# First FFN of a two-layer flow step: block sums moved among the products, a NAT split moved, norm factors in one step

## The chip, the cores and the metric

The program runs on one core of a Trainium2 chip. The metric is the device time of one execution in microseconds (us). The core has a matrix engine (TensorE, PE in the rows; PEld is its weight load), a vector engine (VectorE, DVE), an activation engine (ScalarE, ACT), a general engine (GpSimd, POOL) and a queue that issues transfers (SyncE, SP). [...]

## The reference, cut to what matters

Two layers; each adds half an FFN, a mixer of three attentions (MLA, differential, neighbourhood = NAT) and half an FFN again to `x`, for 128 context and 512 latent tokens of width 1024. The weights are the same for both kinds of token; the shifts, scales and gates come from a conditioning vector and differ.

```
def half_ffn(x, g, shift, scale, gate, w_gate, w_up, w_down):
    h = rmsnorm(x, g) * (1.0 + scale) + shift
    return x + 0.5 * gate * ((silu(h @ w_gate) * (h @ w_up)) @ w_down)

for l in range(2):
    sh1, sc1, g1, sh2, sc2, g2, sh3, sc3, g3 = split(silu(c) @ w_ada[l] + b_ada[l], 9)
    x = half_ffn(x, ffn1_norm[l], sh1, sc1, g1, ffn1_w_gate[l], ffn1_w_up[l], ffn1_w_down[l])
    h = modulate(rmsnorm(x, mix_norm[l]), sh2, sc2)
    x = x + g2 * (concat(MLA(h), DIFF(h), NAT(h)) @ w_out[l])
    x = half_ffn(x, ffn2_norm[l], sh3, sc3, g3, ffn2_w_gate[l], ffn2_w_up[l], ffn2_w_down[l])
y = rmsnorm(x, final_norm)
```

## The kernel before

All 640 tokens lie along the free axis and the 1024 features on 8 tiles of 128 partitions (`x[d]`). Each matrix product in float32 accuracy is three products of rounded operands: operands are split into a high part (a cast on ACT) and a low part (a subtraction on DVE), `mm3` multiplies high by high, high by low and low by high. Weights come in slabs of 512 KB (`raw`, 4 buffers) through the SP queue; `W.get` splits them a number of slots ahead (`W.la`).

An FFN works on two halves of 320 tokens (g = 0, 1). Its first pairs of columns are computed plainly (`plain`, `gu`: 8 x 3 products of 320 columns each). All further pairs are computed by a scheme that replaces eight block products by seven (`seven`: A11, S2, S1, S3, A12, S4, A22). It needs sums of blocks of the activations, T1 to T4, made by `Boundary.blocks(k)` for k = 0 to 3: four sums on DVE and four splits (ACT cast, DVE subtraction) for each k, 32 DVE instructions of 320 columns in all. `plain` calls them after its first half. After each chunk of pairs `down` adds the down-projection to `x`; its results and those of `seven` are read from PSUM by DVE.

The first FFN of layer 0 has an opening of its own, since nothing is loaded yet: for each d from 0 to 7 `begin(d)` computes shift and scale of that feature tile from 1 MB of weights (`begin_sums`: 16 small products, `begin_vectors`: the column sums by `sel` into the PSUM tile `shift`, then `ada_bias` on DVE), applies them to the normed input (`begin_input` in three steps: product with the norm factor; shift and scale and cast; low part), and `first(k)` puts the products of one feature tile behind the preparation of the next. In this stage every instruction is held to program order on its engine (`e.pin`). The modulated input y is a temporary here, so `blocks` first rebuilds it for this FFN as high + low: 16 additions on POOL.

Besides, the modulation of the later stages is computed as background on DVE (`BG`): 112 steps during the first FFN, each of which reads one 256 KB load with two reductions of 512 columns. `BG.tick` earns `RATES[0]` of a step at each product of `seven` and each part of `down`, and three times that (`EARLY`) after each `gu` of the first FFN.

In the mixer a planner (`Plan`) orders chains of work by estimated times. `prompt_n(i)` ends with `finish_o`, the split of one NAT output of 640 columns (ACT cast, DVE subtraction); it waits until 11 units have begun and the projections ckv, cq, d0, d1, dv are done. `mla_v` (named mv) multiplies the compressed keys by one weight slot.

`Norm.stats` turns token sums of squares into factors: a reciprocal root on POOL and a diagonal matrix by one DVE instruction for each 80 or 128 tokens; `bcast` spreads it by a product with ones.

Of the kernel before, what the change touches and what calls it, by code (L numbers as in the profile page):

```python
# [41 lines left out]
LA = {"ffn": 4, "fast": 4, "attn": 1, "edge": 7}  # L42
# [3 lines left out]
FLIGHT, SPLIT = 5, 11  # L46
# [7 lines left out]
EARLY = 3  # L54
RATES = 0.517, 0.339, 0.423, 0
# [272 lines left out]
def build(tc, I, O):  # L328
# [243 lines left out]
    class Norm:  # L572
# [14 lines left out]
        def stats(self):  # L587
# [8 lines left out]
            for j in range(nt):  # L596
                V.tensor_scalar(self.dg[:w, j * w:(j + 1) * w], ident[:w, :w], rs[:w, j:j + 1], None, ALU.mult)
# [5 lines left out]
        def apply(self, d, h, lo, sc, sh, y=None, E=V, Y=V):  # L603
# [4 lines left out]
            E.tensor_tensor(xn, self.bc, x[d][:, self.c0:self.c1], ALU.mult)  # L608
            yield
            for a, b, v in parts(self.c0, self.c1):  # L610
                o, i = y[:, a - self.c0:b - self.c0], xn[:, a - self.c0:b - self.c0]
                if v == 0:
                    A.activation(o, i, AF.Identity, bias=sh[:, d, v:v + 1], scale=sc[:, d, v:v + 1])
                else:
                    Y.tensor_scalar(o, i, sc[:, d, v:v + 1], sh[:, d, v:v + 1], ALU.mult, ALU.add)
            A.copy(h, y)
            yield
            E.tensor_tensor(lo, y, f32(h), ALU.subtract)
# [7 lines left out]
    class Boundary:  # L626
# [3 lines left out]
        def __init__(self, l, w):  # L630
# [3 lines left out]
            self.hT, self.B, self.Y = {}, {}, {}  # L634

# [10 lines left out]
        def apply(self, g, d, E=V, keep=True):  # L646
# [7 lines left out]
            else:  # L654
                k, b = d % 4, d // 4
                h, lo = self.pair(f"B{b + 1}{g + 1}", k)
                if keep:
                    if (g, k) not in self.Y:
                        t = T()
                        self.Y[g, k] = t[:, :NQ], t[:, NQ:]  # L660
                    y = self.Y[g, k][b]
            return n.apply(d, h, lo, adav[self.l][:, i + 1], adav[self.l][:, i], y, E)
# [53 lines left out]
    def ffn(l, w, bound, nbound, first=None):  # L716
        W.la = 0 if first else LA["ffn"]
        aT, sil, both = {}, {}, []
        gate = adav[l][:, 2 if w == "f1" else 8]
# [1122 lines left out]
```

## Time and profile before

| | |
|---|---|
| median of 3 runs | 2736.33 us (2736.01 to 2740.82) |
| profiled execution | 2733.88 us, of which the span of the profile is 2732.1 us |
| PE busy | 2566.5 us, 94% of the span |
| DVE busy | 2019.7 us, 74% |
| ACT busy | 1202.0 us, 44% |
| POOL busy | 592.9 us, 22% |
| mean granted clock of TensorE | 0.974 |

The first FFN of layer 0 fills the span from its start to about 480 us, the mixer of layer 0 the time to about 930 us. Busy times are averages over stages with different limits: the stage tells which engine is waited for. Times in the rows are microseconds from the start of the span; a row merges like instructions that follow each other, with the idle time before it and what ended it in brackets.

### The profile page before, as it was taken

What the parts mean: (1) busy time and instruction counts of PE and PEld (TensorE: products, weight loads), DVE (VectorE), ACT (ScalarE), POOL (GpSimd) and SP (SyncE); (2) the same over time, 40 slices, a digit from 0 to 9 for tenths busy, and PEclk for the clock granted to TensorE, in tenths of its full rate; (3) what the DMA queues carried; (4) which work ended last, traced back from release to release, by engine and by line L of the source; (5) the groups of instructions that cost most, each with busy time, mean ns of one, the idle gap of its engine ahead of it and who ended that gap; (6) DMA issues with size and microseconds to landing.
All of it is one profiled execution on the core that took longest, in us unless ns stands there. A gap on an engine that the chain in (4) does not pass through costs nothing. (4 is left out here: it accounts for less than half of the span.)

```text
span 2732.1 us, 46623 instructions
## 1 busy us (share of the span) xinstructions
PE 2566.5 (94%) x17216; PEld 2429.6 (89%) x17216; DVE 2019.7 (74%) x4542; ACT 1202.0 (44%) x2618; POOL 592.9 (22%) x618
## 2 busy tenths in 40 slices
PE   5799999999989999999999999999988898999998
PEld 5799999977867899999999999998777788999998
DVE  4999999633476799888779999965345669666665
ACT  4333334454366553333453333335445666333441
POOL 0322222012223122222112222301122312222220
PEclk9899999999989999999999999999999899999999
DMA  6376666221321346665436665632213212545441
GB/s 243 119 207 197 199 199 172 95 88 58 93 53 42 117 131 182 172 172 163 140 78 185 197 177 165 182 103 79 89 54 90 54 63 80 144 122 137 123 120 39
DMA packets 144819, 349.73 MB, mean 128 GB/s; under 512 B 18496, under 2 KB 21472, under 8 KB 144592
## 3 DMA queue, kind: packets, MB, share of 16 engines
q1 hardware_dynamic: 119616, 302.28, 34.1%
q0 software_dynamic: 23392, 42.97, 9.6%
q8 instruction: 136, 2.23, 0.3%
q10 hardware_dynamic: 1584, 1.50, 0.2%
q14 instruction: 91, 0.75, 0.1%
HBM read 330.27 MB, written 4.36 MB: 122 GB/s over the span
## 5 line engine op out<-in xcount | busy, mean ns | idle before, releaser
L272 PE MATMUL q<-t,u 128*128 128x320 f32 (+2 forms) x8448 | 1369.3, 315 | 42.9 <-DVE t L272 27.8
L272 PEld LDWEIGHTS q<-t,u 128*128 128x128 f32 x8448 | 1272.2, 191 | 72.8 <-issue 26.0
L272 DVE TENSOR_TENSOR u<-raw,u 128x512 fp32r<-128x512 f32 (+1 forms) x668 | 489.1, 738 | 126.5 <-ACT u L272 80.6
L272 ACT CAST u<-raw 128x512 fp32r<-128x512 f32 (+1 forms) x668 | 400.7, 616 | 362.3 <-PE q L272 150.5
L272 PE MATMUL s<-t,u 128*128 128x320 f32 (+2 forms) x3008 | 515.7, 323 | 24.5 <-ACT u L272 9.2
L272 PEld LDWEIGHTS s<-t,u 128*128 128x128 f32 (+1 forms) x3008 | 450.9, 192 | 44.6 <-ACT t L272 10.5
L272 PE MATMUL p<-t,u 128*128 128x320 f32 (+1 forms) x2936 | 458.8, 315 | 6.0 <-DVE v L272 5.8
L272 PEld LDWEIGHTS p<-t,u 128*128 128x128 f32 (+1 forms) x2936 | 427.4, 186 | 19.5 <-issue 8.6
L272 DVE CUSTOM_DVE_ANT_0 u<-u,u 128x512 f32<-128x512 f32 x512 | 393.0, 771 | 15.8 <-PE q L272 6.1
L272 DVE SCALAR_TENSOR_TENSOR t<-q,adav,t 128x192 f32<-128x192 f32 (+3 forms) x568 | 235.1, 436 | 118.2 <-PE q L272 117.6
L272 POOL TENSOR_TENSOR u<-raw,raw 128x512 f32<-128x512 f32 x78 | 131.5, 1685 | 474.0 <-PE q L272 149.0
L272 ACT CAST u<-u 128x512 fp32r<-128x512 f32 x234 | 144.8, 619 | 194.8 <-PE q L272 83.0
L272 DVE TENSOR_TENSOR u<-u,u 128x512 fp32r<-128x512 f32 (+2 forms) x265 | 194.1, 732 | 43.2 <-PE q L272 11.8
L272 ACT ACTIVATE t<-t 128x320 f32<-128x320 f32 (+2 forms) x168 | 92.4, 553 | 183.5 <-DVE t L272 180.0
L272 POOL DMA_DIRECT2D raw<-in_W x78 | 68.7, 880 | 476.8 <-DVE t L272 186.3
L272 PE MATMUL q<-u,t 128*128 128x256 f32 (+1 forms) x1086 | 152.9, 298 | 18.8 <-ACT u L272 11.5
L272 PEld LDWEIGHTS q<-u,t 128*128 128x128 f32 x1086 | 143.1, 203 | 24.4 <-ACT u L272 13.5
L272 ACT CAST t<-t 128x320 fp32r<-128x320 f32 (+3 forms) x155 | 78.4, 544 | 104.3 <-DVE t L272 102.8
L272 POOL TENSOR_TENSOR u<-u,raw 128x512 f32<-128x512 f32 x78 | 120.3, 1542 | 17.5 <-DVE u L272 7.4
L272 POOL DMA_DIRECT2D u<-in_W x78 | 76.7, 983 | 188.0 <-DMA u<-in_W 54.6
L272 POOL TENSOR_TENSOR sm<-sm,mhalf 128x1 f32<-128x1 f32 (+5 forms) x37 | 33.1, 895 | 380.7 <-DVE sm L272 379.2
L272 DVE TENSOR_TENSOR v<-p,v 128x320 f32<-128x320 f32 x195 | 94.1, 483 | 20.5 <-PE p L272 19.5
(168 smaller groups left out, 2080.3 us busy)
## 6 DMA issues: line engine op xcount, KB each, us to landing
raw<-in_W SPq DMA_DIRECT2D x330, 512.0 KB, 4.0
u<-in_ADA SPq DMA_DIRECT2D x272, 256.0 KB, 4.5
u<-in_W SPq DMA_DIRECT2D x78, 256.0 KB, 4.2
raw<-in_W POOLq DMA_DIRECT2D x78, 256.0 KB, 5.1
u<-in_W POOLq DMA_DIRECT2D x78, 256.0 KB, 5.8
t<-t SPq DMA_DIRECT2D x80, 80.0 KB, 2.1
t<-in_nbias SPq DMA_DIRECT2D x16, 320.0 KB, 5.0
u<-u SPq DMA_DIRECT2D x80, 64.0 KB, 2.0
```

Of the source, the lines that this page charges most:

```text
L272: r = f(*a, **k)
```

## The change

Five edits. The modulated input of the first FFN is kept (8 tiles of 640 columns), and the 16 POOL additions go. `blocks` becomes a generator of 20 steps; in the first FFN, steps are taken at feature tiles 5, 6 and 7 of the opening (`SUMS0`: 2, 3, 5) and after the plain products (`SUMS1`), where 12 background steps are placed too (`STEPS1`) in place of 3 ticks per product; later ticks earn 0.53. The weight lookahead in the plain part is 1. In the opening, both products by `sel` come ahead of the two `ada_bias`, and `begin_vectors` and `begin_sums` ahead of the first step of `begin_input(d + 1)`. `prompt_n` splits its output when mv is done too, and no longer counts units. The diagonal factors of a norm are one TENSOR_TENSOR.

```diff
-LA = {"ffn": 4, "fast": 4, "attn": 1, "edge": 7}
+LA = {"first": 1, "ffn": 4, "fast": 4, "attn": 1, "edge": 7}
-EARLY = 3
-RATES = 0.517, 0.339, 0.423, 0
+SUMS0 = {5: 2, 6: 3, 7: 5}
+SUMS1 = 1, 1, 1, 1, 1, 1, 2, 2, 0, 0
+STEPS1 = 0, 0, 1, 1, 1, 1, 2, 2, 2, 2
+RATES = 0.53, 0.339, 0.423, 0
...
-            for j in range(nt):
-                V.tensor_scalar(self.dg[:w, j * w:(j + 1) * w], ident[:w, :w], rs[:w, j:j + 1], None, ALU.mult)
+            V.tensor_tensor(self.dg[:w].rearrange("p (a b) -> p a b", a=nt),
+                            ident[:w, :w].unsqueeze(1).to_broadcast([w, nt, w]),
+                            rs[:w].unsqueeze(2).to_broadcast([w, nt, w]), ALU.mult)
...
         def blocks(self, k):
-            if (0, k) in self.Y:
-                y11, y21 = self.Y.pop((0, k))
-                y12, y22 = self.Y.pop((1, k))
-            else:
-                y11, y12, y21, y22 = [T(NQ) for i in range(4)]
-                for t, b in ((y11, "B11"), (y12, "B12"), (y21, "B21"), (y22, "B22")):
-                    h, lo = self.pair(b, k)
-                    G.tensor_tensor(t, f32(h), f32(lo), ALU.add)
+            y11, y21 = self.Y.pop((0, k))
+            y12, y22 = self.Y.pop((1, k))
...
+            yield
             for n, t in (("T2", y22), ("T1", y11), ("T3", y12), ("T4", y21)):
                 h, lo = self.pair(n, k)
                 A.copy(h, t)
                 V.tensor_tensor(lo, t, f32(h), ALU.subtract)
+                yield
...
-            if first:
-                BG.tick(EARLY)
+            if sums:
+                for i in range(sums.pop(0)):
+                    next(bound.steps)
+                for i in range(early.pop(0)):
+                    BG.step()
...
-            yield (lambda: state["begun"] >= SPLIT and all(map(plan.done, ("ckv", "cq", "d0", "d1", "dv"))),)
+            yield (lambda: all(map(plan.done, ("ckv", "cq", "d0", "d1", "dv", "mv"))),)
...
         for v in range(2):
             PE.matmul(shift[:, d, v], t[:, v], sel, start=True, stop=True)
+        for v in range(2):
             ada_bias(0, v, d, d + 1, shift[:, d, v].unsqueeze(1))
...
-        begin_input(d + 1)
         if d:
             begin_vectors(d)
             if d + 1 < ND:
                 begin_sums(d + 1)
+        begin_input(d + 1)
...
+        if d in SUMS0:
+            for e in engines:
+                e.pin = None
+            for i in range(SUMS0[d]):
+                next(b.steps)
+            for e in engines:
+                e.pin = tc.keep_in_program_order
```

DVE in the opening, one feature tile, before: `v<-t_170,t` is the first step of an input, `adav` the shift and scale, `u<-raw,u` the low part of a weight slot, `t<-v,t` the low part of an input.

```order
L272 TENSOR_TENSOR v_526<-t_170,t_81 128x320
L272 TENSOR_TENSOR v_529<-t_170,t_81 128x320
L272 TENSOR_TENSOR adav_91<-p_113,bada 128x2 x2
L272 SCALAR_TENSOR_TENSOR adav_91<-adav_91,vec 128x2
L272 TENSOR_TENSOR u_557<-raw_398,u_556 128x512
L272 TENSOR_SCALAR v_467<-v_466,adav_91 128x128
L272 TENSOR_TENSOR t_461<-v_464,t_461 128x320
L272 TENSOR_TENSOR t_462<-v_467,t_462 128x320
```

The same tile's stretch after.

```order
L276 TENSOR_TENSOR adav_91<-p_113,bada 128x2 x2
L276 SCALAR_TENSOR_TENSOR t_211<-t_211,t_209 128x320
L276 SCALAR_TENSOR_TENSOR adav_91<-adav_91,vec 128x2
L276 TENSOR_TENSOR v_546<-t_170,t_81 128x320
L276 TENSOR_TENSOR v_548<-t_170,t_81 128x320
L276 TENSOR_TENSOR u_551<-raw_398,u_550 128x512
L276 TENSOR_SCALAR t_252<-v_487,adav_91 128x128
L276 SCALAR_TENSOR_TENSOR t_209<-t_211,t_209 128x320
L276 TENSOR_TENSOR t_483<-t_250,t_483 128x320
L276 TENSOR_TENSOR t_252<-t_252 128x320
L276 TENSOR_TENSOR t_484<-t_252,t_484 128x320
L276 TENSOR_TENSOR t_565<-t_211,t_565 128x320
```

The shift and scale now stand ahead of the first step of the next input, and steps of the block sums (`t_211`, `t_209`, `t_565`) stand between the input's own instructions.

POOL behind the opening, before: the sums of weight blocks, then the first of the 16 additions that rebuild y.

```order
L272 DMA raw_696<-in_W 128x512
L272 DMA u_698<-in_W 128x512
L272 TENSOR_TENSOR u_966<-raw_696,raw_701 128x512
L272 TENSOR_TENSOR u_967<-u_966,raw_701 128x512
L272 TENSOR_TENSOR v_999<-t_208 128x320
L272 TENSOR_TENSOR v_1000<-t_209 128x320
L272 TENSOR_TENSOR v_1001<-t_400 128x320
```

POOL at the same place after.

```order
L276 DMA raw_830<-in_W 128x512
L276 DMA u_832<-in_W 128x512
L276 TENSOR_TENSOR u_974<-raw_830,raw_835 128x512
L276 TENSOR_TENSOR u_975<-u_974,raw_835 128x512
L276 DMA raw_1289<-in_W 128x512
L276 DMA u_1291<-in_W 128x512
L276 TENSOR_TENSOR u_1478<-raw_1289,raw_1294 128x512
```

The 16 additions are gone; POOL has only its transfers and the sums of weight blocks there.

DVE in the mixer of layer 0, before: four splits of NAT outputs (`t<-t,t` of 640 columns) stand ahead of the low part of the slab that mv reads (`u_8872<-raw_8869`).

```order
L272 TENSOR_TENSOR t_8803<-u_8796,t_8802 128x512
L272 TENSOR_REDUCE sm_8899<-s_1847_8895 128x1
L272 TENSOR_TENSOR t_8810<-t_6590,t_8809 128x640
L272 TENSOR_TENSOR t_8814<-t_6917,t_8813 128x640
L272 TENSOR_TENSOR t_8818<-t_7397,t_8817 128x640
L272 TENSOR_TENSOR t_8822<-t_7760,t_8821 128x640
L272 TENSOR_TENSOR u_8872<-raw_8869,u_8871 128x512
L272 TENSOR_REDUCE sm_8906<-s_1850_8902 128x1
```

DVE after: the four splits stand behind mv's weights (16 rows further on) and shortly ahead of the first update from the output projection (`t_75<-q`).

```order
L276 SCALAR_TENSOR_TENSOR t_8922<-t_8929,sm_8935,t_8922 128x640
L276 TENSOR_TENSOR t_8945<-t_6547,t_8944 128x640
L276 TENSOR_TENSOR t_8949<-t_6874,t_8948 128x640
L276 TENSOR_TENSOR t_8953<-t_7354,t_8952 128x640
L276 TENSOR_TENSOR t_8957<-t_7717,t_8956 128x640
L276 TENSOR_REDUCE sm_8985<-s_1869_8981 128x1
L276 STREAM_SHUFFLE u_9003<-t_8960 128x512
L276 TENSOR_TENSOR u_9004<-t_8960,u_6028 128x512
L276 RECIPROCAL sm_8988<-sm_8787 128x2
L276 SCALAR_TENSOR_TENSOR t_75<-q_9021,adav_91,t_75 128x320
```

The rows moved behind mv's weight split and stand now between the scores of differential units and the first output update.

## Rows read from the trace of the kernel before

**Rows 1.** who PE waited for, 0 to 140 us: total, times, longest

```profile
PE p L272 <- DVE adav L272: 6.2, 6, 1.5
```

**Rows 2.** timeline of PE in the opening: start, duration, what [idle before]

```profile
31.00 0.59 PE L272 MATMUL p<-sel,v 128*128 128x2 f32 x2 [2.79 <-DMA u<-in_ADA]
...
59.06 0.28 PE L272 MATMUL p<-sel,v 128*128 128x2 f32 x2
60.79 0.38 PE L272 MATMUL p<-sel,v 128*128 128x2 f32 x2 [1.45 <-DVE adav L272]
...
62.11 0.71 PE L272 MATMUL s<-t,u 128*128 128x320 f32 x3
...
70.94 0.60 PE L272 MATMUL s<-t,u 128*128 128x320 f32 x3
```

**Rows 3.** timeline of DVE, one feature tile of the opening

```profile
59.37 0.49 DVE L272 TENSOR_TENSOR t<-v,t 128x320 fp32r<-128x320 f32 x1 [0.45 <-ACT t L272]
59.78 0.89 DVE L272 TENSOR_TENSOR v<-t,t 128x320 f32<-128x320 f32 x2
60.58 0.15 DVE L272 TENSOR_TENSOR adav<-p,bada 128x2 f32<-128x2 f32 x1
```

**Rows 4.** timeline of ACT, first and last of one feature tile

```profile
56.46 0.37 ACT L272 COPY v<-p 128x256 f32<-128x256 f32 x1 [2.91 <-PE p L272]
...
58.88 0.46 ACT L272 CAST t<-v 128x320 fp32r<-128x320 f32 x1
```

**Rows 5.** windows: stretch, length, PE PEld DVE ACT POOL busy (count), clock, DMA share, GB/s

```profile
72.20:112.50 40.30, 37.47 (x240) 36.73 (x240) 37.50 (x71) 10.56 (x25) 21.84 (x19) 0.96 0.59 181
112.50:140.00 27.50, 14.72 (x81) 13.49 (x81) 26.26 (x69) 9.97 (x22) 1.98 (x2) 0.75 0.21 66
140.00:470.00 330.00, 320.36 (x2151) 315.16 (x2150) 326.84 (x765) 116.29 (x218) 82.07 (x68) 1.00 0.68 194
```

**Rows 6.** timeline of PE from the plain pass to the first seven

```profile
101.83 3.68 PE L272 MATMUL q<-t,u 128*128 128x320 f32 x24
105.35 3.68 PE L272 MATMUL s<-t,u 128*128 128x320 f32 x24
...
121.80 0.90 PE L272 MATMUL s<-t,u 128*128 128x320 f32 x2 [9.24 <-ACT u L272]
...
125.78 3.03 PE L272 MATMUL s<-t,u 128*128 128x320 f32 x10 [2.82 <-DVE u L272]
```

**Rows 7.** timeline of POOL, first and last of the 16 additions

```profile
90.08 13.56 POOL L272 TENSOR_TENSOR v<-t 128x320 f32<-128x320 f32 x11
...
110.20 4.28 POOL L272 TENSOR_TENSOR v<-t 128x320 f32<-128x320 f32 x4 [0.43 <-DVE t L272]
```

**Rows 8.** timeline of DVE under and after the additions

```profile
80.43 0.68 DVE L272 CUSTOM_DVE_ANT_0 u<-u,u 128x512 f32<-128x512 f32 x1
...
108.96 6.68 DVE L272 TENSOR_TENSOR t<-v,t 128x320 fp32r<-128x320 f32 x8
...
117.57 1.68 DVE L272 TENSOR_TENSOR t<-v,t 128x320 fp32r<-128x320 f32 x4
```

**Rows 9.** waits of PE, 140 to 560 us

```profile
PE q L272 <- DVE t L272: 6.3, 11, 1.6
```

**Rows 10.** waits of the SP queue, 60 to 140 us

```profile
SPq L272 <- DVE u L272: 31.0, 6, 10.3
```

**Rows 11.** timeline of ACT, NAT splits and mv's weights in layer 0

```profile
777.83 2.60 ACT L272 CAST t<-t 128x640 fp32r<-128x640 f32 x4
780.34 0.61 ACT L272 CAST u<-raw 128x512 fp32r<-128x512 f32 x1
```

**Rows 12.** timeline of PE, the first product of mv

```profile
781.27 1.01 PE L272 MATMUL q<-u,t 128*128 128x256 f32 x3 [5.09 <-ACT u L272]
```

**Rows 13.** timeline of DVE, factors of the norm ahead of layer 0's second FFN

```profile
957.14 2.80 DVE L272 TENSOR_SCALAR v<-ident,sm 80x80 f32<-80x80 f32 x4 [1.22 <-POOL sm L272]
```

**Rows 14.** timeline of DVE, factors ahead of layer 1

```profile
1376.85 0.77 DVE L272 TENSOR_SCALAR v<-ident,sm 80x80 f32<-80x80 f32 x4 [1.15 <-POOL sm L272]
```

More of the change, by code (lines that the diff above doesn't have):

```diff
@@ L607, in apply @@
                 y = T(self.n)
-            E.tensor_tensor(xn, self.bc, x[d][:, self.c0:self.c1], ALU.mult)
+            V.tensor_tensor(xn, self.bc, x[d][:, self.c0:self.c1], ALU.mult)
             yield
@@ L614, in apply @@
                 else:
-                    Y.tensor_scalar(o, i, sc[:, d, v:v + 1], sh[:, d, v:v + 1], ALU.mult, ALU.add)
+                    V.tensor_scalar(o, i, sc[:, d, v:v + 1], sh[:, d, v:v + 1], ALU.mult, ALU.add)
             A.copy(h, y)
             yield
-            E.tensor_tensor(lo, y, f32(h), ALU.subtract)
+            V.tensor_tensor(lo, y, f32(h), ALU.subtract)
             yield
@@ L634, in __init__ @@
             self.hT, self.B, self.Y = {}, {}, {}
+            self.steps = (None for k in range(4) for _ in self.blocks(k))
         def require(self):
@@ L644, in pair, with apply @@
             return self.B[n, k][:, :NQ], self.B[n, k][:, NQ:]
-        def apply(self, g, d, E=V, keep=True):
+        def apply(self, g, d):
             n = self.norms[g]
@@ L656, in apply @@
                 h, lo = self.pair(f"B{b + 1}{g + 1}", k)
[L657 to L662, printed above, removed]
-        def blocks(self, k):
-            if (0, k) in self.Y:
-                y11, y21 = self.Y.pop((0, k))
-                y12, y22 = self.Y.pop((1, k))
-            else:
-                y11, y12, y21, y22 = [T(NQ) for i in range(4)]
-                for t, b in ((y11, "B11"), (y12, "B12"), (y21, "B21"), (y22, "B22")):
-                    h, lo = self.pair(b, k)
-                    G.tensor_tensor(t, f32(h), f32(lo), ALU.add)
+                if (g, k) not in self.Y:
+                    t = T()
+                    self.Y[g, k] = t[:, :NQ], t[:, NQ:]
+                y = self.Y[g, k][b]
+            return n.apply(d, h, lo, adav[self.l][:, i + 1], adav[self.l][:, i], y)
+        def blocks(self, k):
+            y11, y21 = self.Y.pop((0, k))
+            y12, y22 = self.Y.pop((1, k))
             V.tensor_tensor(y11, y11, y12, ALU.subtract)
@@ L718, in ffn @@
         aT, sil, both = {}, {}, []
+        sums, early = (list(SUMS1), list(STEPS1)) if first else ([], [])
         gate = adav[l][:, 2 if w == "f1" else 8]
@@ L817, in plain @@
             for g in halves:
-                W.la = 0 if g == halves[0] else LA["ffn"]
+                W.la = (LA["first"] if first else 0) if g == halves[0] else LA["ffn"]
                 for f in (f0, f0 + 1):
@@ L827, in plain @@
                     post(f, g, up)
-                if g == halves[0]:
+                if g == halves[0] and not first:
                     with ahead():
-                        for k in range(4):
-                            bound.blocks(k)
+                        for _ in bound.steps:
+                            pass
         if first:
@@ L1659, in begin_input @@
             if d not in steps:
-                steps[d] = [b.apply(g, d, V, False) for g in range(2)]
+                steps[d] = [b.apply(g, d) for g in range(2)]
             for st in steps[d]:
@@ L1685, in first @@
                 e.pin = None
-            W.la = LA["ffn"]
+            W.la = LA["first"]
             BG.open(LIMITS[0], RATES[0])
```

4 lines of the change are left out of this document (2 added, 2 removed).

## The prediction

> **What bounds the kernel now.** I read the waits of the matrix engine first, then the stretches in which it waits, engine by engine. Behind the first FFN's plain pass the matrix engine is nearly always either at work or waiting for the vector engine, so I ask of each stretch which of the two ends last.
>
> The opening (to 71.5 us). For each feature tile PE runs the second product by `sel` only after DVE has read the first one's result: six such waits, 6.2 us in all [rows 1], 1.45 us in a typical tile [rows 2]. An earlier one of 2.79 us is put down to a transfer [rows 2], but the same instruction waits there for the same read on DVE. The reader sees why on DVE: the read (`adav`) stands behind the two first-step products of the next input, which stand behind the last low part of this one [rows 3]. So every tile is one serial loop through PE, ACT and DVE.
>
> The plain pass and the first seven products (72.2 to 140). PE issues 321 products there [rows 5]. Undisturbed, 24 of them take 3.52 us (starts at 101.83 and 105.35, [rows 6]), or 0.147 us each; 321 need 47.1 us, and the two windows last 67.8. So 20.7 us are lost: 9.24 and 2.82 us of idle time in a row where the first seven products wait for weight splits [rows 6], smaller waits before, and slow products after them (the granted clock is 0.75 on average in the second window, 0.96 in the first, [rows 5]; a mean between full speed and the lower of the two levels, half of it). DVE is busy 37.5 + 26.3 = 63.8 us of the 67.8 [rows 5]: it is what ends last.
>
> The rest of the first FFN (140 to 470). DVE is busy 326.8 of 330 us, PE 320.4 [rows 5]; PE's largest wait there is 6.3 us for results that DVE reads out [rows 9]. Both are at their limit.
>
> **The change part by part**
>
> *Opening.* Both `sel` products now stand together and `adav` stands ahead of the next input. The 6.2 and 2.79 us go: 9.0 us. What is late next? Between the end of the small products of tile d + 1 (PE reaches the products at 62.11, [rows 2]) and the products of tile d + 1 itself, PE has the 18 products of the tile before (18 x 0.147 = 2.6 us) and the next tile's `sel` and small products (0.28 from the row at 59.06, 62.11 - 60.79 = 1.32, together 1.6 us, [rows 2]): 4.2 us. ACT and DVE need from 56.46 [rows 4] to 59.86 (59.37 + 0.49, [rows 3]) for the same, 3.4 us. So they are covered by 0.8 us. The block sums put in here are one DVE instruction of 320 columns in a tile at first, 0.42 us (four in 1.68, [rows 8]), which fits the 0.45 us that DVE waits for ACT between two low parts [rows 3]. In tile 7 the cover is gone: three casts of block sums stand on ACT ahead of the tile's own casts, 3 x 0.46 us [rows 4] = 1.4 us. Gain 9.0 - 1.4 = 7.6 us; bounds 0 (if the loop through ACT sets the period after all) and 9.0.
>
> *Sums moved, additions gone.* While POOL does its 16 additions (13.56 us for the first eleven, 4.28 for the last four, [rows 7]), a DVE low part takes 6.68 / 8 = 0.83 us against 0.42 without them [rows 8]: DVE does half its work in about 19 us (17.8 in the two rows, 1.2 for the sixteenth by the mean of the eleven), so the additions cost it 9.5 us. Of the 32 instructions of the block sums, 22 now stand ahead of the plain pass, where DVE waits: 22 x 0.42 = 9.2 us. Three half-steps of background fewer stand ahead of the first update of x: 3 x 0.6 = 1.8 us (a half-step: its reduction lasts 0.68 us, of which some 0.6 to the next instruction, [rows 8]). DVE's 63.8 us become 63.8 - 9.5 - 9.2 - 1.8 = 43.3, below PE's 47.1. So PE sets this stretch, the seven find their weights split, and with no idle time in front of them the clock has no reason in these rows to fall. Of 20.7 us lost I leave 1.0 for small gaps at the ends of halves: gain 19.7. Bounds: 20.7; and 11, if DVE, which cannot run ahead of results that PE still has to make, idles about 8 us in the pass and then is late for the seven by that.
>
> *Later in the first FFN.* The later ticks earn 0.53 for 0.517, and the 1.8 us of background taken from the front come back here, where DVE is full [rows 5]: -1.8. And nine instructions of some 0.6 us stand on DVE between the last result of the seven and the first update of x, 5.4 us, while PE can fill two PSUM banks with parts of twelve products, 3.5 us, before it waits: a loss of 1.9, against one of 0.4 that I would give the old order there, so -1.5. Together -3.3, bounds -8 (DVE's whole backlog comes back) and 0.
>
> *NAT split.* In each layer four casts of 640 columns, 2.60 us, stand on ACT ahead of the cast of mv's weights [rows 11], and PE waits 5.09 us for that cast [rows 12]. They go behind: PE starts 2.6 us earlier. But they now stand in front of the first output product, between scores of differential units, where the vector engine's four subtractions go with them. I take 1.0 a layer, 2.0 in all; bounds +2.6 and -2.6 a layer.
>
> *Factors in one step.* Four instructions of 80 columns take 0.77 us [rows 14], but 2.80 while POOL sums weights beside them [rows 13]. One TENSOR_TENSOR of 320 columns takes 0.42, or 0.83 beside POOL [rows 8]. So 0.35 or 2.0 us less. Six such norms (the second token group of each boundary) are on the path; if two are slow ones: 4 x 0.35 + 2 x 2.0 = 5.4, of which I keep 3.0, since PE's products of the stage before still cover part. Bounds 0 and 5.4.
>
> [...]
>
> Sum: 7.6 + 19.7 - 3.3 + 2.0 + 3.0 = 29.0 us. The profiled execution took 2733.9 (span 2732.1 and 1.8 around it), so 2704.9; the median of the runs lies 2.4 us above that execution, so 2707 us.
>
> **Rivals**
>
> *DVE is the bound in the plain pass after all.* For it: it was busy 63.8 of 67.8 us there [rows 5]. Against it: 43.3 against 47.1 us. The opening's gain would then be eaten by waiting, the moved work gives 20.5 less the 8 us of idle above, 12.5, and with the last two parts less 1.5 in the rest: 12.5 + 5.0 - 1.5 = 16, 2720 us.
>
> *The opening keeps its period.* If ACT and DVE need 4.3 us and more where I count 3.4, the loop closes there and the 7.6 us go: 21.4, 2715 us. Against it: ACT sat idle 2.91 us in a tile [rows 4].
>
> *The sums are still late.* The change keeps eight more tiles of 640 columns. If a block sum must wait for a tile that the plain pass frees at its end, the sums stand where they stood, and the seven wait for them as before: left are the last two parts, 5.0 us: 2731 us. Against it: the order shows most sums far ahead.
>
> *The SP queue holds back the background loads (slower).* The twelve early background steps stand on DVE between the weight splits, and their loads stand on SP behind three slabs, each of which waits for a buffer that DVE frees. Before, SP waited up to 10.3 us for such a buffer [rows 10]. If each of the three slabs costs DVE such a wait, 31 us, DVE is late by 31 us for the splits behind, and the change ends at -29 + 31 = +2, in a bad case more; with the extra idle clock time after it, some +8: 2744 us. It decides from three waits of 10 us on. Against it: the slabs' buffers are read out several instructions ahead of the first step that needs a load.
>
> **How the numbers follow.** Forecast (22 to 38 us gained): 0.60. DVE bound: 0.22. Opening unchanged: 0.08. Sums late: 0.06. SP queue: 0.04. About 0.2% (5.5 us) is what a measurement of this kernel tells from no change. The first three cases are faster, 0.90; sums late is within it, 0.06; the SP queue slower, 0.04. The range 2697 to 2724 holds the forecast with the better ends of its parts, the opening and the DVE cases with 4 us beyond; it leaves out the last two cases and the tails.
>
> **What would show it.** The first product of the plain pass starts near 64.5 us instead of 72.25; no wait for `adav` is left in the opening; the first seven start about 35 us later with no wait above 2 us, at a granted clock of 1.0; POOL has no additions of 320 columns there. If instead DVE is full from 64 us and PE waits for split weights before the seven, the first rival's sum holds. In the mixer the first product of mv should wait under 3 us, and the six norm steps show one DVE instruction of 0.4 to 0.9 us. A first FFN that ends less than 12 us earlier would make the prediction wrong.

## The result, and the profile after

The changed kernel takes 2697.9 us (median of 4 runs, 2696.2 to 2706.2) against 2736.2 us of the kernel before on the same chip (median of 4): ratio 0.9884, 95% interval 0.9861 to 0.9906. The forecast was 2707 us. The two profiled executions lie 34.7 us apart (2733.9 and 2699.2); the forecast gain was 29.0.

Stage by stage, in us. Each norm gives PE two products with a matrix of ones for each token group: a column sum, then the spreading of the factors. An FFN or a mixer ends here with the first column sum of the norm behind it; a stretch "norms behind it" ends with the spreading for the second token group. The first FFN ends at 516.2 us before, not at about 480 as I wrote ahead of the prediction.

| stage | before | after | difference | forecast |
|---|---|---|---|---|
| first FFN, to its first norm | 516.2 | 491.0 | -25.3 | -24.0 |
| mixer of layer 0, with the norms ahead of it | 414.9 | 412.1 | -2.8 | -1.0 |
| norms behind it | 28.9 | 26.6 | -2.2 | -3.0 for all norms |
| second FFN, layer 0 | 414.8 | 415.7 | +0.9 | 0 |
| norms behind it | 33.3 | 31.7 | -1.6 | see above |
| first FFN, layer 1 | 434.5 | 436.1 | +1.7 | 0 |
| mixer of layer 1, with the norms ahead of it | 417.8 | 410.6 | -7.2 | -1.0 |
| norms behind it | 28.7 | 26.6 | -2.1 | see above |
| second FFN, layer 1, and the end | 443.1 | 446.9 | +3.8 | 0 |

The differences are taken before rounding.

The opening and the plain pass, timeline of PE in the changed kernel (start, duration, what, idle time before it in brackets), which answers to [rows 2, 6]:

```profile
45.99 0.50 PE L276 MATMUL p<-sel,v 128*128 128x2 f32 x4
...
50.17 0.50 PE L276 MATMUL p<-sel,v 128*128 128x2 f32 x4
...
59.27 0.41 PE L276 MATMUL s<-t,u 128*128 128x320 f32 x1 [1.68 <-ACT t L276]
...
63.93 7.30 PE L276 MATMUL q<-t,u 128*128 128x320 f32 x48
...
95.71 3.68 PE L276 MATMUL q<-t,u 128*128 128x320 f32 x24
99.23 1.92 PE L276 MATMUL s<-t,u 128*128 128x320 f32 x12
...
118.57 5.05 PE L276 MATMUL q<-t,u 128*128 128x320 f32 x24 [3.34 <-DVE t L276]
```

The four `sel` products stand together, no wait for `adav` is left, and a tile takes 4.18 us (50.17 - 45.99) instead of 5.3 to 5.8 in the later tiles. The last tile waits for ACT's casts of block sums, and behind that wait the granted clock (the share of its full speed that PE was allowed) is down: 0.57 from 60 to 64 us. The plain pass starts at 63.93 instead of 72.25, the first seven at 99.23 without a wait. A new wait of 3.34 us stands ahead of the first down product.

Windows of the changed kernel (stretch, length, busy us and count of PE, PEld, DVE, ACT and POOL, clock, DMA share, GB/s), against [rows 5]:

```profile
63.90:110.90 47.00, 46.98 (x321) 46.97 (x321) 42.54 (x104) 19.56 (x43) 5.02 (x4) 1.00 0.57 171
110.90:491.00 380.10, 366.56 (x2442) 360.29 (x2440) 360.83 (x840) 133.86 (x248) 82.96 (x68) 1.00 0.63 183
```

The 321 products that took 67.8 us before take 47.0. DVE is busy 42.5 us there and no longer the one that ends last. From there to the end of the first FFN it is 380.1 us, against 376.2 before (140.0 to 516.2): 3.9 are given back.

PE at the product of mv that waits in layer 0, against [rows 12]:

```profile
748.24 1.12 PE L276 MATMUL q<-u,t 128*128 128x256 f32 x6
...
753.75 1.01 PE L276 MATMUL q<-u,t 128*128 128x256 f32 x3 [2.57 <-ACT u L276]
```

The wait went from 5.09 to 2.57 us. But it is not what the prediction took it for. mv makes six blocks of three products, and the row of six products ahead of the wait is its first two blocks, so its weights were ready by then. In the kernel before, PE and ACT read:

```profile
773.25 1.11 PE L272 MATMUL q<-u,t 128*128 128x256 f32 x6
...
780.86 0.36 ACT L272 COPY u<-q 128x256 f32<-128x256 f32 x1
```

The product of [rows 12], at 781.27, begins mv's third block. It starts 0.05 us after ACT has copied the first block's result out of PSUM (780.86 + 0.36 = 781.22; in the changed kernel the copy ends at 753.69 and the product starts at 753.75). The slab that is cast at 780.34 [rows 11] is a later one: its low part is ready on DVE only at 783.67, behind the third block. The four NAT casts stood ahead of that copy as much as ahead of the cast, so taking them away shortens the wait by the same 2.5 us.

DVE at three norms; the first row stands against [rows 13], the second against [rows 14], the third is the second token group ahead of layer 1:

```profile
928.08 1.56 DVE L276 TENSOR_TENSOR v<-ident,sm 80x320 f32<-80x320 f32 x1 [1.22 <-POOL sm L276]
...
1347.47 0.49 DVE L276 TENSOR_TENSOR v<-ident,sm 80x320 f32<-80x320 f32 x1 [1.15 <-POOL sm L276]
...
1375.48 1.55 DVE L276 TENSOR_TENSOR v<-ident,sm 80x320 f32<-80x320 f32 x1 [1.15 <-POOL sm L276]
```

One instruction stands for each group of two to four. It takes 0.43 to 0.56 us in nine of the twelve norm steps, but 1.56 in the three beside POOL's sums, not the 0.4 to 0.9 that I had named.

### The profile page after: what moved, and what is told of

The parts are those of the page before. It is cut to its first block, busy times and chain, and to the rows that moved or that the text cites. A ratio compares the mean times of both kernels' runs of the same rounds, so it can differ in the third digit from the quotient of the medians.

```text
span 2697.4 us, 46603 instructions
## 1 busy us (share of the span) xinstructions
PE 2551.2 (95%) x17216; PEld 2413.8 (89%) x17216; DVE 2011.5 (75%) x4515; ACT 1203.1 (45%) x2618; POOL 568.0 (21%) x602
## 5 line engine op out<-in xcount | busy, mean ns | idle before, releaser
L276 PE MATMUL q<-t,u 128*128 128x320 f32 (+2 forms) x8448 | 1362.4, 314 | 45.5 <-DVE t L276 31.8
L276 DVE CUSTOM_DVE_ANT_0 u<-u,u 128x512 f32<-128x512 f32 x512 | 384.8, 756 | 12.8 <-PE q L276 7.6
L276 POOL TENSOR_TENSOR u<-raw,raw 128x512 f32<-128x512 f32 x78 | 125.6, 1610 | 477.0 <-DVE part L276 141.9
L276 PEld LDWEIGHTS q<-u,t 128*128 128x128 f32 x1086 | 142.1, 202 | 19.3 <-ACT u L276 8.8
L276 ACT CAST t<-t 128x320 fp32r<-128x320 f32 (+3 forms) x187 | 92.2, 530 | 96.9 <-DVE t L276 95.0
L276 DVE TENSOR_TENSOR t<-t,t 128x320 fp32r<-128x320 f32 (+4 forms) x210 | 116.3, 587 | 11.4 <-ACT t L276 9.2
```

The source lines that it names most:

```text
L276: r = f(*a, **k)
```

## Experiments

Times are medians; the ratio is to the kernel before in the same session. The repeat of the changed kernel is the nearest yardstick; it ran in one session with three of the experiments (the early NAT split, the four factors, the shared gate). In the other experiments' sessions the kernel before lay between 2728.3 and 2731.5 us, against 2732.3 there, so differences of a few us between sessions tell little.

**The changed kernel again.** No edit.

> The changed kernel once more, unchanged, on the same chip as the three others: how far its stages repeat. Expected: the first FFN ends at 491 us within 3, the mixers keep their lengths within 2 us, 2698 in all. If instead the mixers differ by 4 us and more from one profile to the next, their gain over the kernel before is at least in part the clock's chance.

2700.0 us, ratio 0.9883 (0.9867 to 0.9899). The first FFN ended at 492.7, the mixers took 412.5 and 411.4 us (412.1 and 410.6 in the first profile). But the second FFN of layer 0 took 420.1 instead of 415.7. So stages of an FFN differ by up to 4.4 us between two profiles of one kernel, and the +0.9, +1.7 and +3.8 of my table are within that. Yet the last stage takes 444.2 to 447.3 us in all twelve profiles of the changed kernel and its variants, and 443.1 and 443.3 in the two of the kernel before and its variant: there 1 to 4 us may be the change's own, and why is not known. The two mixers repeat within 0.8 us; over the seven kernels that share this mixer code they take 410.6 to 413.6.

**The opening's old order.**

```diff
-        for v in range(2):
             ada_bias(0, v, d, d + 1, shift[:, d, v].unsqueeze(1))
...
+        begin_input(d + 1)
         if d:
             begin_vectors(d)
...
-        begin_input(d + 1)
```

> The changed kernel with the opening's old order (next input ahead of the vectors, each sel product followed by its read); the block sums stay in tiles 5 to 7. Theory (serial loop through PE, ACT and DVE in each tile): the waits for adav come back, the plain pass starts at about 72 us instead of 63.9, everything behind it keeps its own length, and the end is 7.6 to 8.3 us later, about 2706. Rival (the vector engine is the bound of the whole first FFN, so what the opening gives is given back behind it): the plain pass starts late but the first FFN ends at most 2 us later, about 2699.

2712.0 us, ratio 0.9932 (0.9910 to 0.9954): 12.0 more than the repeat. The plain pass starts at 75.73 us, 11.8 later than in the changed kernel, and the first FFN ends 13.0 us later (11.2 later than in the repeat). Timeline of PE:

```profile
61.05 0.38 PE L276 MATMUL p<-sel,v 128*128 128x2 f32 x2 [1.85 <-DVE adav L276]
...
67.25 0.38 PE L276 MATMUL p<-sel,v 128*128 128x2 f32 x2 [1.85 <-DVE adav L276]
...
75.33 0.56 PE L276 MATMUL s<-t,u 128*128 128x320 f32 x2 [0.79 <-ACT v L276]
...
86.00 3.68 PE L276 MATMUL q<-t,u 128*128 128x320 f32 x24
```

The mechanism holds and the rival falls: nothing of the opening is given back. The size was too small, since in the old loop the block sums lengthen the last tiles (waits of 1.85 instead of 1.45 us, and a late last tile), while the new order has more room for them.

**The opening's new order alone, in the kernel before.**

```diff
+        for v in range(2):
             ada_bias(0, v, d, d + 1, shift[:, d, v].unsqueeze(1))
...
-        begin_input(d + 1)
         if d:
             begin_vectors(d)
...
+        begin_input(d + 1)
```

> The kernel before with the opening's new order alone (sums, additions, NAT splits and factors as before). Theory (my sum: 7.6 us of the opening stand by themselves, since all of DVE's later work shifts with the plain pass): 7 to 8.5 us faster than before, about 2728.5, with the plain pass starting near 64 us. Rival (DVE is the bound in the pass, 63.8 of 67.8 us busy, so the gain is eaten by waits ahead of the seven): within 3 us of before, with waits ahead of the seven that are longer by what the opening gives.

2719.8 us, ratio 0.9959 (0.9941 to 0.9977); in the profile the first FFN ends 14.6 us earlier. PE starts the plain pass 14.8 us earlier than before:

```profile
46.90 0.50 PE L272 MATMUL p<-sel,v 128*128 128x2 f32 x4
51.09 0.50 PE L272 MATMUL p<-sel,v 128*128 128x2 f32 x4
...
57.44 7.31 PE L272 MATMUL q<-t,u 128*128 128x320 f32 x48 [0.47 <-DVE v L272]
```

Of the 14.8, 1.1 are the start of the program and some 2.9 the products of the first tile (three of them in 0.71 us here, in 1.17 us before), so about 10.8 belong to the order. All of it arrives at the end of the first FFN, against the rival that DVE would eat it, and by the medians the whole run is 11.7 us shorter, where I had expected 7 to 8.5.

**The additions on POOL again**, at the new places of the sums.

```diff
+                for t, b in ((y11, "B11"), (y12, "B12"), (y21, "B21"), (y22, "B22")):
+                    h, lo = self.pair(b, k)
+                    G.tensor_tensor(t, f32(h), f32(lo), ALU.add)
```

> The changed kernel with the 16 POOL additions back (the first input is not kept, the sums rebuild it), at the places of the spread sums: 12 additions in the opening and 4 in the plain pass. Theory (the additions cost because DVE runs at half rate beside them, and hurt only where DVE is full): DVE's instructions of 320 columns beside them take 0.8 us instead of 0.42; of the 9.5 us in my sum some 1 to 5 show, since 12 of the additions lie where DVE idles: 2699 to 2703. Rival (they cost 9.5 us wherever they stand): about 2707. Second rival (POOL and DVE do not disturb each other, the long low parts of before were something else): instructions stay at 0.42 to 0.49 us and the time at 2698.

2706.6 us, ratio 0.9916 (0.9891 to 0.9941): 6.6 more than the repeat; the first FFN ends 8.3 us later than in the changed kernel, 6.5 later than in the repeat. POOL and DVE of this kernel (timelines):

```profile
55.07 4.41 POOL L276 TENSOR_TENSOR v<-t 128x320 f32<-128x320 f32 x4 [4.99 <-ACT v L276]
```

```profile
50.82 0.48 DVE L276 TENSOR_TENSOR t<-v,t 128x320 fp32r<-128x320 f32 x1
...
56.51 4.12 DVE L276 TENSOR_TENSOR t<-v,t 128x320 fp32r<-128x320 f32 x5
```

Five low parts beside the additions take 0.82 us each, against 0.42 in a row without them [rows 8]. It is the first rival that comes nearer: the additions cost 6.5 to 8.3 of my 9.5 us although twelve stand in the opening, where the plain pass starts 5.4 us later (69.36 against 63.93). There too DVE is part of the loop: the last tiles wait 1.70 us for DVE and 1.10 for ACT, and the granted clock is 0.50 from 60 to 66 us, against 0.72 in the changed kernel.

**The block sums late**, the input still kept.

```diff
-SUMS0 = {5: 2, 6: 3, 7: 5}
-SUMS1 = 1, 1, 1, 1, 1, 1, 2, 2, 0, 0
+SUMS0 = {}
+SUMS1 = 0, 0, 0, 0, 0, 0, 0, 0, 0, 0
...
-                if g == halves[0] and not first:
+                if g == halves[0]:
```

> The changed kernel with the block sums where the kernel before had them, behind the first half of the plain pass at high priority; the first input is still kept, so the POOL additions stay away. The sixteen subtractions find room in the opening by themselves, the sixteen low parts stand in one piece ahead of the seven's weight splits. Theory (most of the gain of this part is the additions that are gone and the half of the sums that lies in the opening): the pass has 6 x 0.42 = 2.5 us more on DVE, 45.4 against PE's 47.1, and the bunch makes PE wait 1 to 4 us ahead of the first seven: 2699 to 2702. Rival (the even spreading earns the 9.2 us of my sum in full): 9 us later, about 2707, with waits for split weights of more than 5 us ahead of the seven. Other rival (the additions were all of it): no change, 2698.

2700.3 us, ratio 0.9895 (0.9871 to 0.9920): no difference from the repeat that can be measured. In the profile the first FFN ends 2.8 us later, 5.7 if the first tile's products had been as slow as in the changed kernel (three in 0.71 us against 1.17). Two profiles below with the sums spread and an equally quick first tile (the early NAT split, the four factors) end it at 488.2 and 488.7, this one at 493.8. The waits of PE, 0 to 160 us (total, times, longest):

```profile
PE q L276 <- DVE t L276: 8.3, 2, 8.0
```

The wait does not come ahead of the seven, as I had written, but ahead of the first down product. Sixteen subtractions went into the opening by themselves, so this undoes half the spreading. The spreading is worth a few us by the profiles, nothing that the medians show; the additions and the opening are the larger parts.

**The NAT split at its old place.**

```diff
-            yield (lambda: all(map(plan.done, ("ckv", "cq", "d0", "d1", "dv", "mv"))),)
+            yield (lambda: state["begun"] >= 11 and all(map(plan.done, ("ckv", "cq", "d0", "d1", "dv"))),)
```

> The changed kernel with the old condition for the NAT split (from the eleventh unit on, not behind mv). Theory (the split's place decides the wait of mv's first product, and the clock falls behind that wait and the next ones): mv's first product waits 5.1 us again instead of 2.6, products behind it last twice as long for 15 to 25 us in each layer, and the two mixers end 3 and 7 us later than in the changed kernel: 2708. Rival (only the wait counts, the term of my sum): 2 to 5 us in all, 2700 to 2703. Other rival (the mixers' gain is the clock's own doing, the same from run to run only by chance): no change within 2 us in either mixer.

2706.0 us, ratio 0.9898 (0.9879 to 0.9917): 6.0 more than the repeat. The mixers take 416.1 and 418.8 us, 4.0 and 8.1 more than in the changed kernel; mv's third block waits 5.09 again. Waits alone don't explain it: the windows that begin with that block, 50 us long, in this kernel (both layers) and in the changed one:

```profile
753.20:803.20 50.00, 43.11 (x207) 34.12 (x207) 34.36 (x70) 28.95 (x75) 10.82 (x15) 0.77 0.26 67
...
2081.00:2131.00 50.00, 43.10 (x207) 34.12 (x207) 34.28 (x70) 28.88 (x74) 10.83 (x15) 0.77 0.26 66
```

```profile
753.80:803.80 50.00, 40.80 (x211) 31.07 (x212) 37.07 (x74) 32.05 (x80) 10.82 (x15) 0.87 0.28 72
...
2075.60:2125.60 50.00, 40.64 (x217) 30.85 (x217) 37.87 (x76) 32.74 (x81) 10.28 (x15) 0.90 0.28 72
```

PE is busier with the split early and yet does fewer products, 207 against 211 and 217: the granted clock is 0.77 instead of 0.87 and 0.90, so it spends more of the stretch at the lower level (the records of the granted clock in the traces of the kernel before and of the changed one hold two levels, 1.00 and 0.50; so it is twice the missing share: 46% against 26% and 20%).

**Idle products ahead of mv**, with the NAT split early and with it late.

```diff
+                for i in range(0 if j else 40):
+                    PE.e.matmul(ps, ch, M["ck"][0][:, 0:256], start=True, stop=True)
                 PE.matmul(ps, ch, wh, start=True, stop=False)
```

> The NAT split early as in the kernel before (the run e3), with 40 idle products of 256 columns ahead of mv's first product, in the 5.1 us of its wait. It tells the wait from the clock: the wait itself stays. Theory (of the 4 and 8 us that the early split costs in the mixers, more than half is the clock): the two mixers end 5 us or more earlier in all than in e3, about 2700. Rival (the waits of the late order are the cost: mv, and the output products behind the split): no change within 2 us in all, 2706.

2696.4 us, ratio 0.9880 (0.9856 to 0.9904). The six runs spread from 2686.3 to 2705.0, and the profiled one, 2690.1, is the second shortest; the interval overlaps that of the run without idle products, so the medians alone do not settle it. In the profile the mixers take 407.1 and 406.9 us: 9.0 and 11.9 less than without the idle products, and less than in the changed kernel. Timeline of PE, and windows from mv's third block on as above:

```profile
750.27 5.03 PE L1255 MATMUL q<-t 128*128 128x256 f32 x40
755.13 0.52 PE L276 MATMUL q<-u,t 128*128 128x256 f32 x3
...
758.32 0.62 PE L276 MATMUL q<-u,t 128*128 128x256 f32 x3 [1.06 <-ACT u L276]
```

```profile
758.30:808.30 50.00, 41.62 (x254) 32.06 (x255) 38.91 (x81) 36.14 (x93) 12.65 (x18) 1.00 0.26 67
...
2072.50:2122.50 50.00, 41.62 (x255) 32.03 (x256) 38.90 (x81) 36.12 (x93) 12.68 (x18) 1.00 0.26 66
```

The idle products stand ahead of mv's first block, not in the wait: they push the first two blocks, which had not waited, behind them, and so fill the time in which PE would have waited for the third. The third block starts where it did, 264.8 us into the mixer of layer 0 against 265.1, so nothing useful is done sooner. But behind it the clock stays at 1.00 and 254 products are done in the same 50 us.

> The changed kernel with 20 idle products of 256 columns (their results are overwritten) ahead of mv's first product, in the 2.6 us in which PE waits there. Theory (PE's clock falls behind waits, and part of the mixers' time is products at half speed): the products of the 8 us behind mv take 0.11 us instead of 0.27 each, and each mixer ends 1.5 to 3 us earlier: about 2695. Rival (the clock is of no account there, since other engines set the pace behind mv): the products are fast and then wait, no change within 1 us a layer, 2700 as in the repeat. Second rival (the idle products hold mv up): later by what they take beyond the wait, at most 2.5 us a layer, 2705.

With 20 instead of 40 idle products, in the changed kernel: 2698.7 us, ratio 0.9888 (0.9867 to 0.9909), no measurable difference. The mixer of layer 0 was 3.7 us shorter, that of layer 1 was 3.5 longer: there the clock fell ahead of mv and again behind it. A later run has the same 20 idle products (the block sums one tile earlier, below): its mixers take 414.3 and 411.2, so the gain in layer 0 did not repeat.

The mixers in three parts (us, layer 0 / layer 1): to mv's first product or the idle ones ahead of it, from there to mv's third block, and from there to the mixer's end; behind them the time at the lower level in that last part, and in the whole mixer, by the records of the granted clock in the traces:

| kernel | to mv | to its third block | to the end | of it at the lower level | length | of it at the lower level |
|---|---|---|---|---|---|---|
| before | 257.0 / 258.8 | 8.0 / 8.0 | 149.9 / 150.9 | 27 / 30 | 414.9 / 417.8 | 41 / 48 |
| before, opening alone | 256.6 / 259.2 | 8.0 / 8.0 | 151.1 / 151.2 | 30 / 30 | 415.8 / 418.3 | 44 / 51 |
| NAT split early | 257.0 / 259.6 | 8.0 / 8.0 | 151.1 / 151.2 | 30 / 30 | 416.1 / 418.8 | 44 / 51 |
| changed | 257.3 / 256.8 | 5.5 / 5.5 | 149.3 / 148.3 | 16 / 14 | 412.1 / 410.6 | 31 / 27 |
| changed, again | 257.5 / 257.1 | 5.5 / 5.5 | 149.5 / 148.8 | 16 / 16 | 412.5 / 411.4 | 31 / 31 |
| changed, 20 idle products | 256.9 / 259.4 | 5.5 / 5.5 | 145.9 / 149.2 | 7 / 14 | 408.4 / 414.1 | 20 / 34 |
| the same, sums earlier | 259.7 / 256.6 | 5.5 / 5.5 | 149.1 / 149.1 | 14 / 14 | 414.3 / 411.2 | 34 / 27 |
| NAT split early, 40 idle products | 256.8 / 256.8 | 8.0 / 8.0 | 142.3 / 142.1 | 3 / 3 | 407.1 / 406.9 | 17 / 17 |
| NAT split early, idle at two places (below) | 254.7 / 259.7 | 8.0 / 8.0 | 142.4 / 142.2 | 3 / 3 | 405.1 / 409.9 | 3 / 17 |

Three things can be read from it. The place of the split sets the second part: 8.0 us or 5.5. The third part goes with the clock: with the early split it is 150 to 151 us, and 142.1 to 142.4 in all four mixers in which 40 idle products kept the clock up, though the third block started no sooner. And the first part does not depend on the split: where the clock falls once more ahead of mv, as in layer 1 of the kernel before, mv is reached at 258 to 260 us instead of 257 to 258. That happens with the late split too (in both layers of the runs with the old opening and with the four factors). So the early split costs 2.5 us of waiting in each layer, and about 2 us behind it, where the clock is down longer (the third part is 150.9 us on average over the three kernels with the early split, 148.7 over the seven with the late one and no idle products); the rest of the difference in layer 1, 2.0 of 7.2 us, is not its own.

**Four factors.**

```diff
-            V.tensor_tensor(self.dg[:w].rearrange("p (a b) -> p a b", a=nt),
...
+            for j in range(nt):
+                V.tensor_scalar(self.dg[:w, j * w:(j + 1) * w], ident[:w, :w], rs[:w, j:j + 1], None, ALU.mult)
```

> The changed kernel with four instructions of one source for the factors of a norm instead of one of two sources. Theory (the number of instructions weighs more than the rate, most of all beside POOL's sums): the waits ahead of the two second-group norms that were slow go back from 1.9 to 2.85 us, others by 0.35, and the end is 2 to 4 us later: about 2701. [...] Other rival (PE's products of the stage before cover the step): no change, 2698.

2700.3 us, ratio 0.9884 (0.9867 to 0.9901): by the medians no difference from the repeat. In the profile the three stretches of norms between stages take 28.9, 31.8 and 28.1 us against 26.6, 31.7 and 26.6, so 4.0 us more. DVE there:

```profile
928.43 2.79 DVE L276 TENSOR_SCALAR v<-ident,sm 80x80 f32<-80x80 f32 x4 [1.22 <-POOL sm L276]
...
1378.08 1.78 DVE L276 TENSOR_SCALAR v<-ident,sm 80x80 f32<-80x80 f32 x4 [1.15 <-POOL sm L276]
```

The new form is the faster one in these rows: 1.56 and 1.55 us against 2.79 and 1.78 beside POOL's sums, 0.49 against 0.77 without them. The whole time cannot tell a gain of 3 to 4 us from the spread of the runs (2697.1 to 2702.9 in the repeat).

**Half a gate's background steps moved to the second FFN.**

```diff
-RATES = 0.53, 0.339, 0.423, 0
+RATES = 0.49, 0.381, 0.423, 0
...
+                half = ND // 2 if self.todo[0] == (0, 8) else 0
```

> A version meant to be faster: half of the background steps for layer 0's last gate (8 of its 16 half-steps, 9.8 us of DVE) go from the first FFN, where DVE is busy 325 of 328 us behind the plain pass, to the second FFN, where it is busy 298 of 345. Theory (DVE is the bound of the first FFN): the first FFN ends 6 to 9 us earlier and the second one at most 1 us later: about 2691. Rival (PE is as much the bound there, its 12 us of idle time are single waits at the first down products and elsewhere): within 3 us of 2698, with DVE's idle time higher by the 9.8 us.

2699.4 us, ratio 0.9880 (0.9863 to 0.9898): nothing that the medians show. The window of the first FFN behind the first down products:

```profile
123.00:440.00 317.00, 309.14 (x2071) 305.06 (x2070) 306.55 (x706) 113.32 (x210) 75.80 (x63) 0.99 0.65 184
```

DVE now has 10.5 us of idle time, against 3.0 in such a window of the changed kernel (313.97 us busy of 317, from 128 us on), but PE is busy for the same 309 us. The first FFN ends at 486.0 us; the two profiles with an equally quick first tile (the early NAT split, the four factors) end it at 488.2 and 488.7. So the rival holds: less work on DVE alone brings some 2 us, not 6 to 9, and "both are at their limit" was right.

**Block sums one tile earlier, with 20 idle products.**

```diff
-SUMS0 = {5: 2, 6: 3, 7: 5}
+SUMS0 = {4: 2, 5: 3, 6: 3, 7: 2}
```

> A version meant to be faster: the 20 idle products, and the block sums one tile earlier (2, 3, 3 and 2 steps in tiles 4 to 7 instead of 2, 3 and 5 in 5 to 7), so that the last tile, where PE waited 1.7 us for ACT and then ran slowly, has three steps fewer. Theory: the plain pass starts 1 to 2.5 us earlier, all else as in the run with the idle products alone: 2693 to 2695. Rival (tiles 4 to 6 have no room either, 4.18 us of PE against DVE and ACT with the sums): the pass starts at the same time or later, 2698 and more.

2697.7 us, ratio 0.9883 (0.9863 to 0.9903); 2693 to 2695 were expected. From the first small product (2.1 us later than in the run with the idle products alone) to the end of the first FFN it is 476.9 against 477.5 us: no gain. The last tiles still wait for ACT (1.22 and 0.78 us).

**Idle products at two places, NAT split early.**

```diff
+                if tag == "ckv" and j == 0:
+                    idle = {3: (4, 9), 6: (9, 5)}.get(k, (0, 0))
```

> A version meant to be faster than both: the run with the early NAT split and 40 idle products, with 27 more idle products (128 x 256, results thrown away) in the waits of the first latent product (0.6, 1.1 and 0.6 us near 640 us of the first mixer), behind which 15 us go at the lower clock in every kernel so far. Theory (the clock is lost to those waits): the stretch from 640 to 656 runs at full clock and each mixer is 2 to 4 us shorter than 407 us; in all about 2690. Rival (those waits keep their length and the clock falls through others, the transposes that wait 1.3 us for POOL among them): mixers of 407 us or 1 to 2 us more, 2696 to 2700.

2692.1 us, ratio 0.9858 (0.9823 to 0.9892), the shortest of all, though its interval overlaps that of the changed kernel; its four runs (2689.7 to 2693.8) all lie below the five of the repeat (2697.1 to 2702.9), which ran in another session. The stretch around 646 us in layer 0, in this kernel and in the changed one:

```profile
640.00:656.00 16.00, 12.09 (x103) 11.22 (x101) 5.86 (x18) 9.63 (x29) 5.88 (x10) 1.00 0.20 66
```

```profile
638.00:654.00 16.00, 12.93 (x63) 11.81 (x64) 5.90 (x19) 8.03 (x25) 5.91 (x10) 0.57 0.19 66
```

The clock is 1.00 instead of 0.57, with a wait of 2.18 us for POOL still in it. The mixer of layer 0 takes 405.1 us with 3 us at the lower level; that of layer 1 takes 409.9 with 17, since there the clock fell nevertheless, around 1958 us and once more ahead of mv. So a mixer can be up to 7 us shorter than in the changed kernel, but not in every layer and run.

## Why the prediction was right, and where a term was mis-sized

- *Opening.* 7.6 forecast, 8.3 in the trace (72.25 to 63.93), 0.9 of it the start. The period of 4.2 us, set by PE, came out as 4.18. Inside the term two sizes were off in opposite directions, so it is partly luck that the sum came out so well. The order alone is worth 10.8 rather than 9.0. The block sums cost some 3.3 rather than the 1.4 that I gave them: the last tile's wait of 1.68 us, and the lower clock behind it, of which no term spoke. The case "the opening keeps its period" is out.
- *Sums moved, additions gone.* 19.7 forecast; 67.8 - 47.0 = 20.8. DVE's load of 43.3 us came out as 42.5, PE's 47.1 as 47.0, so the case "DVE is the bound" is out, and the run with the opening alone shows that not even before did DVE eat the opening's gain. The additions cost 6.5 to 8.3 us by the run that puts them back (9.5 forecast), the half of the sums that the run with the late sums undoes is worth 5 to 6 by the profiles. That the sums are late, or that SP's queue holds the loads back, shows nowhere: there is no wait ahead of the seven. SP itself still waits for buffers that DVE frees, up to 7.0 us from 60 to 140 us.
- *Later in the first FFN.* -3.3 forecast, -3.9 in the trace, with the wait ahead of the first update where it was expected (3.34 us and two small ones, ahead of the down products).
- *NAT split.* This is the mis-sized term: 2.0 us in all, with bounds of 2.6 a layer, against 2.8 and 7.2 in the trace and 4.0 and 8.1 in the run that undoes it; by the parts of the mixers about 4.6 a layer are the split's own. The reading was wrong in one place: what waits is mv's third block, for a copy on ACT, and not its first for the cast of its weights. The 2.5 us came out all the same, because the same four casts stood ahead of both. The step that failed is the price of the new place, a loss of 1.6 a layer. The new place did bring new waits (1.55 and 1.85 us), and yet the mixer behind mv's third block became shorter, by about 2 us: PE spent 14 to 16 us there at the lower clock instead of 27 to 30. I had priced waits by their lengths alone and had read the clock only in the first FFN. In the mixer it stood in the same rows: the three products in [rows 12] take 1.01 us, the three of the run with idle products 0.62.
- *Factors in one step.* 3.0 forecast, about 4 by the profiles: 2.2 and 2.1 in the two stretches behind the mixers, 2.3 and 1.6 when undone; too small for the medians. The 1.6 of the stretch between the layers are not this edit's: with four instructions it takes 31.8 us too in two other profiles. The duration that I named was wrong: the instruction takes 1.56 us where POOL sums weights beside it, not 0.83, and three norms are slow, not two.
- *Other stages.* 6.4 us longer in three FFNs, which I had put at nothing. For two of them the repeat shows such differences without any edit; for the last one it stays open whether the change lengthens it.

Sum by the profiles: 25.3 + 9.9 + 5.9 - 6.4 = 34.7, against 24.0 + 2.0 + 3.0 = 29.0. The time lies inside the range because the first FFN, four fifths of the forecast, came out within 1.3 us. The mixers gave 7.9 us more than forecast: 6.4 behind mv's third block, where a loss of 3.2 was forecast and a gain of 3.2 came, and 1.7 ahead of mv, where the clock fell once less and nothing shows that the split did it. The norms gave 2.9 more, and the later FFNs took 6.4 back. So the number is nearer than the mechanism of this part deserves.

## What to carry to other kernels

Price a wait of the matrix engine by what the granted clock does behind it, not by its length: here 40 products whose results are thrown away, put just ahead of a wait, let nothing useful start sooner and yet shortened what followed by 9 us in four mixers of two kernels (142.1 to 142.4 us, 3 of them at the lower clock, against 151.1 and 151.2 with 30), while moving the work that caused the wait gave about 4.6. With 20 of them ahead of a wait of 2.6 us the gain did not repeat. When a serial loop is reordered, take the largest of the engines' own sums per turn as its new period; here that sum (4.2 us for PE) forecast the new period to 0.02 us. Work that is put into the idle time of such a loop need not be free: the sums and the additions that looked hidden in the opening cost some 3.3 and 5.4 us there.

## What was not expected of the hardware

- Two short waits, of 0.56 and 1.13 us, stood ahead of a fall of the clock. In the mixer of layer 0 of the changed kernel the granted clock is 1.00 until 640 us and 0.57 over the 16 us from 638 on. The waits there, in the timeline of PE, and two windows:

```profile
636.96 0.45 PE L276 MATMUL q<-u,t 128*128 128x160 f32 x2 [0.56 <-ACT u L276]
638.54 0.34 PE L276 MATMUL q<-u,t 128*128 128x160 f32 x1 [1.13 <-DVE u L276]
...
642.44 0.50 PE L276 MATMUL q<-u,t 128*128 128x160 f32 x1 [1.03 <-DVE u L276]
...
645.19 0.48 PE L276 MATMUL p<-ident,u 128*128 128x128 f32 x1 [1.26 <-POOL u L276]
```

```profile
636.00:640.00 4.00, 2.31 (x17) 1.42 (x14) 2.11 (x7) 2.25 (x7) 1.15 (x2) 1.00 0.05 16
640.00:644.00 4.00, 2.66 (x12) 2.05 (x11) 2.24 (x7) 2.08 (x8) 1.36 (x2) 0.53 0.30 115
```

  From 628 us on, only these two stand ahead of the fall; those of 1.03 and 1.26 come when the clock is down already. With idle products in the first three the clock stays at 1.00 there, a wait of 2.18 us in the same stretch included; in the same stretch of layer 1 it is 0.72 from 1954 to 1964 us, with the same 2.18 us in it. So the runs show no length of a wait from which on the clock falls.
- The kernel before spreads from 2714.8 to 2742.7 us over 44 runs in four sessions, the changed one from 2696.2 to 2706.2 over nine. The runs of the kernel before with the higher mean clock are the shorter ones: those up to 2724 us have a mean clock of 0.980 to 0.983, those from 2734 us on 0.972 to 0.976.
- The first tile's products take either 0.39 or 0.24 us each, which moves the opening by some 2.9 us. A window there shows a granted clock of 1.00 in both cases, but only because the trace has no record of the clock so early. Its first record, at full speed, stands at 32.7 us in the changed kernel, and the products become quick just there (three in 1.00 us at 30.06, three in 0.71 us at 32.46). In all nine profiles with a slow first tile it stands at 32.7 to 36.9 us, and in the five with a quick one at 24.9 to 25.5, ahead of the tile's first product. So this difference too goes with the clock, and a 1.00 ahead of the first record says nothing.
